# The Fourier projection unfolded, two-operand work moved from GpSimd to VectorE, and the splitting of layer 1's weights spread differently

## The chip, the cores and the metric

The kernel runs on one core of one Trainium2 chip. A core has a matrix engine (TensorE, "PE" in the profile; its weight loads are "PEld"), a vector engine (VectorE, "DVE"), an activation engine (ScalarE, "ACT"), a general engine (GpSimd, "POOL") and a queue engine that issues all transfers here (SyncE, "SP"). They run side by side and wait for one another through semaphores. Matmul results land in PSUM, eight banks of 128 x 512 float32 values; everything else is held in SBUF. The metric is the device time of one execution in microseconds (us); lower is better.

## What is computed

The program is a two-layer encoder trunk on one sequence of 512 positions and 1024 channels, in float32. Of the reference, what matters here:

```
for l in range(DEPTH):                                  # 2 layers
    h = rmsnorm(x, norm1[l])
    p = h @ w_in[l]                                     # 512 Fourier columns | 512 q | 128 k | 128 v
    f = jnp.fft.fft2(u, axes=(1, 2), norm="ortho").real # over positions and channels
    y_f = f @ w_f + b_f
    y_a = windowed_gqa(rope(rmsnorm(q)), rope(rmsnorm(k)), v, sink[l])   # 8 heads, |i-j| <= 128
    x = x + concat([rmsnorm(y_f), rmsnorm(y_a)]) @ w_o[l]
    h = rmsnorm(x, norm2[l])
    gate, val = split(dwconv_centred(h @ w_up[l], conv_w[l], conv_b[l]))  # 2 x 2816 columns
    x = x + (silu(gate) * val) @ w_down[l]
```

## The kernel before, in words

**Three matmuls for one.** Float32 operands are split into a high half that the matrix engine takes in its fast float32 form and a low half, the rest: `split` (lines 94 to 101) and `wsplit` (118 to 127) make the high half on ACT and the low half with a two-operand subtraction, by default on DVE. `mm3` (103 to 108) then issues high x high, low x high and high x low. In the profile, lines 106, 107 and 108 are these three, line 86 is any ACT instruction, line 89 any two-operand instruction of DVE or POOL, line 92 any DVE instruction with a scalar as well, since small helpers record them.

**Order.** The program is written as a plain sequence. A scheduler orders each engine's instructions by priority (program order) and by readiness in a simulation with modelled times. Only one order is written by hand: the matmuls of the first half of the output projection are issued after given steps of the attention (`proj`, line 604), as filler.

**Layer 0's mixing.** Activations are kept as eight tiles of 128 channels by 512 positions. `norm_tile` (289) scales a tile by the norm's weights and splits it, and adds its squares to an accumulator (on POOL but for the last). The q, k, v projection (325 to 346) uses these tiles as the stationary operand, in two groups of columns that both take the PSUM tags "mm" x3 and "av"; the norm's factor is put in at the eviction, a scalar for each position.

The Fourier branch uses the symmetry of a cosine and sine transform: it folds the positions (element n with element 512 - n, sums and differences) and the columns before it multiplies. `fold_h` (351) normalises a tile again, now with the factor as a row (`rb1`, line 323), folds it (`fold`, 299: a copy of two elements on DVE, a sum and a difference of 255 elements on POOL) and splits it. The weights are loaded and folded the same way (`load_wu`, 305). The projection (486 to 502) is, for each of eight channel tiles, five pieces of 256 or 258 columns, one of them with a single row. Then come the transform over channels and that over positions (526 to 557, one loop with two stages), the multiplication with the folded Fourier weights (561 to 592), a norm, and the first half of the output projection (619). The attention (436 to 476) goes head by head in 32 steps: scores, maximum on DVE, exponent on ACT, normalising on POOL, transposes on PE, split, product with v. Its result goes through the second half of the output projection (626), each of whose eight rows ends with the next norm's tile.

**Feed-forward.** 44 up projections in two halves of 22 (`HALVES`, line 35), each 24 matmuls of 512 columns with its weights loaded into one of three raw buffers ("wraw") and split, then eviction and a three-tap convolution on ACT and DVE; per pair a silu and a product (line 660, POOL). After each half the down projection: eight rows of 33 matmuls.

**Layer 1's weights ahead of time.** `presplit` (135) is a generator that runs beside layer 0's feed-forward. Each step takes one tile of layer 1's weights, folds it if it is a Fourier one, splits it and stores both halves to a scratch in DRAM. The loads use the same three raw buffers as the feed-forward's. A step is taken after each of the 44 up projections and once after each half (lines 658 and 692). In layer 1 `fetch` (183) loads the halves.

Of the kernel before, what the change touches and what calls it, by code (L numbers as in the profile page):

```python
# [37 lines left out]
def encoder_kernel(tc, t):  # L38
# [28 lines left out]
    def f(x):  # L67
# [4 lines left out]
    TEMPS = {"act": (1024, 8), "m4": (1024, 5), "slab": (1028, 4), "pT": (2560, 2),  # L72
             "tA": (512, 6), "tF": (512, 6), "sq": (512, 2)}
# [61 lines left out]
    def presplit(l):  # L135

        def keep(key, src):
# [4 lines left out]
            return lambda: [nc.sync.dma_start(o, f(z)) for o, z in zip(kept[key], two)]  # L142

        def store(waiting, w):
            if waiting:
                waiting.pop()()
            if w:
                waiting.append(w)

        late = []  # L150
        for grp in (1, 0):
            for kk in range(KT // 2):
                raw = wload(t["w_qkv"][l, grp, kk], 768)
                for i in range(2):
                    store(late, keep(f"qkv{grp}{2 * kk + i}", raw[:, i * 384:(i + 1) * 384]))
                    yield
        for kk in range(KT // 2):
            raw = wtile()
            nc.sync.dma_start(raw.rearrange("p (k c) -> p k c", k=2),
                              t["w_in"][l, 2 * kk * P:2 * (kk + 1) * P, 0:FW].rearrange("(k p) c -> p k c", p=P))  # L160
            for k in range(2):
                w = temp(512, "tA")
                fold(w, raw[:, k * 512:(k + 1) * 512], nc.vector)
                store(late, keep(f"u{2 * kk + k}", w))
                yield
        for j in range(NF):
            raw = wload(t["w_fold"][l, j], 1024)
            w = temp(512, "tA")
            tt(w[:, :256], raw[:, :256], raw[:, 512:768], ALU.add)
            tt(w[:, 256:], raw[:, 256:512], raw[:, 768:], ALU.subtract)  # L170
            store(late, keep(f"f{j}", w))
            yield
        for half in range(2):
            for mp in range(KT // 2):
                raw = wload(t["w_o"][l, half, :, mp * 1024:(mp + 1) * 1024], 1024)
                for i in range(2):
                    store(late, keep(f"o{half}{2 * mp + i}", raw[:, i * 512:(i + 1) * 512]))
                    yield
        store(late, None)
        while True:  # L180
            yield
# [65 lines left out]
    zero = temp(512, "sq")  # L247
    nc.vector.memset(zero, 0.0)
    warm = temp(512, "sq", F32R)
# [19 lines left out]
    def load_tables():  # L269
        for i in range(2):  # L270
            raw = wload(t["dft"][i], 512)
            th = cp.tile([P, 512], F32R, tag=f"th{i}", name=f"th{i}")
            tl = cp.tile([P, 512], F32R, tag=f"tl{i}", name=f"tl{i}")
            split(th, tl, raw)
            tab.append((th, tl))
        alt = wtile()[:1, :258]
# [4 lines left out]
    def add_square(acc, src, first, eng=nc.gpsimd, tag="sq"):  # L281
        if first:
            act(acc, src, AF.Square)
        else:
            sq = temp(512, tag)
            act(sq, src, AF.Square)
            tt(acc, acc, sq, ALU.add, eng)

    def norm_tile(k, g, acc):
# [3 lines left out]
        add_square(acc, x[k], k == 0, nc.gpsimd if k < KT - 1 else nc.vector)  # L293
# [5 lines left out]
    def fold(dst, src, eng):  # L299

        nc.vector.tensor_copy(dst[..., 0:257:256], src[..., 0:257:256])
        tt(dst[..., 1:256], src[..., 1:256], src[..., 511:256:-1], ALU.add, eng)
        tt(dst[..., 257:512], src[..., 1:256], src[..., 511:256:-1], ALU.subtract, eng)

    def load_wu(l, kk):

        raw = wtile()
        nc.sync.dma_start(raw.rearrange("p (k c) -> p k c", k=2),
                          t["w_in"][l, 2 * kk * P:2 * (kk + 1) * P, 0:FW].rearrange("(k p) c -> p k c", p=P))
        out = []  # L310
        for k in range(2):
            w = temp(512, "tA")
            fold(w, raw[:, k * 512:(k + 1) * 512], nc.gpsimd)
            out.append(w)
        return out
# [4 lines left out]
    for l in range(L):  # L320

        r1 = col_rstd(acc, 1.0 / D)
        rb1 = row_rstd(r1)
        qraw = {}
        for grp in (1, 0):
            pq = [psum("mm" if b < 3 else "av") for b in range(NB)]
# [22 lines left out]
        hs = {}  # L349

        def fold_h(k, eng):
            hr = temp(512, "tF")
            hf = temp(512, "tF")
            stt(hr, x[k], g1[:, l, k:k + 1], rb1, ALU.mult, ALU.mult)
            fold(hf, hr, eng)
            hs[k] = pair("slab")
            split(hs[k][:, 0, :], hs[k][:, 1, :], hf)

        for k in range(4):
            fold_h(k, nc.gpsimd)  # L360
# [4 lines left out]
        for i in range(4):  # L365
            tt(ra[:, i], ra[:, i], qkg[:, l, i, None, :].to_broadcast([P, NB, HD]), ALU.mult, nc.gpsimd)
# [5 lines left out]
        def prep(us):  # L372
# [4 lines left out]
            for i, u in enumerate(us):  # L377
                two = temp(1024, "act").rearrange("p (z b h d) -> p z b h d", z=2, **dims)
# [6 lines left out]
            for i, u in enumerate(us):  # L385
# [50 lines left out]
        def attention(p, first_pair):  # L436
# [39 lines left out]
            add_square(accA, py, first_pair, nc.vector if p == 2 else nc.gpsimd)  # L476


        if l == 0:
            load_tables()  # L480
# [4 lines left out]

        pee = [psum(), psum(), psum("av")]
        poo = psum()
        for kk in range(KT // 2):
            if not l:
                wu = load_wu(l, kk)  # L490
            for k in (2 * kk, 2 * kk + 1):
                if k not in hs:
                    fold_h(k, nc.gpsimd)
                w = fetch(f"u{k}") if l else wsplit(wu[k % 2])
                h = hs[k]
                st, sp_ = k == 0, k == KT - 1
                we = [z[:, 0:258] for z in w]
                wo = [z[:, 256:512] for z in w]
                for m, (c0, c1) in enumerate(((0, 128), (128, 256), (256, 257))):
                    mm3(pee[m][:c1 - c0, :258], [h[:, s, c0:c1] for s in range(2)], we, st, sp_)  # L500
                mm3(poo[:, 0:256], [h[:, s, 257:385] for s in range(2)], wo, st, sp_, skip_group_check=True)
                mm3(poo[:127, 256:512], [h[:, s, 385:512] for s in range(2)], wo, False, sp_, skip_group_check=True)
# [7 lines left out]
        def tail_out(pe, scale):  # L510
            b = tp.tile([1, 2, 258], F32R, tag="tail", name=nm("tail"), bufs=2)
# [3 lines left out]
        def stage_out(pe, po, scale):  # L515
            tiles = []
            for m in range(2):
                a = pair("slab", 514)
                n = P - m
                split(a[:, 0, :258], a[:, 1, :258], pe[m][:, :258], scale=scale)  # L520
                split(a[:n, 0, 258:514], a[:n, 1, 258:514], po[:n, m * 256:(m + 1) * 256], scale=scale)
# [3 lines left out]
        ue, ut = stage_out(pee, poo, 1.0)  # L525
        for stage in range(2):
            pe = [psum() for _ in range(2)]
            po = psum()
            pe.append(psum())
# [252 lines left out]
```

## Time and profile before

| | us |
|---|---|
| median of three runs | 1111.37 |
| lowest and highest of them | 1110.5, 1114.45 |
| the profiled execution | 1112.89 |
| its span, from first to last instruction | 1111.1 |
| PE busy | 1068.9 |
| DVE busy | 778.9 |
| ACT busy | 514.5 |
| POOL busy | 278.1 |

The span is one execution, recorded by the profiler. The busy time of an engine is the time in which it had an instruction under way; matmuls are pipelined and their ends modelled, so a busy PE is not necessarily at its peak rate. A group row of the profile reads: line, engine, operation, output<-inputs by the program's names, shapes, count, then busy us and mean ns of one, then the idle time of that engine just before them and what ended it.

### The profile page before, as it was taken

The page shows a single profiled execution, that of the slowest core. Times are in us where ns is not written, and L with a number is a line of the kernel's source. Part 1 is how long each engine was busy: PE and PEld are TensorE (multiplying, and loading weights), DVE is VectorE, ACT ScalarE, POOL GpSimd, SP SyncE. Part 2 cuts the span into 40 slices and gives each one's busy share as a digit, 9 for nine tenths or more (in the row PEclk, how much of TensorE's full clock was granted, in tenths as well). Part 3 has the DMA queues.
Part 4 walks back from the last instruction along what each step waited for, and adds up shares of the span by engine and source line. Part 5 has one row for each costly group of instructions (what it writes and reads, how often), then busy time and mean ns, then how long its engine had stood idle before and what let it go on. Part 6 is the DMA issues. An engine that isn't in the chain of part 4 may idle for free.

```text
span 1111.1 us, 14836 instructions
## 1 busy us (share of the span) xinstructions
PE 1068.9 (96%) x5187; PEld 892.3 (80%) x5187; DVE 778.9 (70%) x1406; ACT 514.5 (46%) x964; POOL 278.1 (25%) x326
## 2 busy tenths in 40 slices
PE   7878899999999999999999899999999999999998
PEld 6776788788888888778889787878888888888887
DVE  8997874988883477887437968477878535787732
ACT  4536763565552244554412676245555323544421
POOL 5678654511010001111105344050201000010100
PEclk9978999999999999999999999999999999999999
DMA  6312113366643576763355510523232333333241
GB/s 218 110 58 95 39 39 119 122 215 229 207 147 93 196 249 232 231 218 105 87 168 174 188 58 20 171 76 95 95 97 82 104 97 97 112 89 101 78 130 59
DMA packets 58574, 141.65 MB, mean 127 GB/s; under 512 B 6521, under 2 KB 19074, under 8 KB 58498
## 3 DMA queue, kind: packets, MB, share of 16 engines
q1 hardware_dynamic: 58498, 140.69, 40.0%
q8 instruction: 41, 0.67, 0.2%
q14 instruction: 35, 0.29, 0.1%
HBM read 117.60 MB, written 23.07 MB: 127 GB/s over the span
## 4 chain that ended last, share of the span: by engine, by line
PE 72%; DVE 15%; DMA 6%; issue 3%; ACT 2%; POOL 1%; SPq 0%; DVEq 0%; POOLq 0%; ACTq 0%
PE ps L106 22%; PE ps L108 22%; PE ps L107 22%; DVE wlo L89 4%; DMA wraw<-in_w_o_dram 3%; DMA wraw<-in_w_fold_dram 2%; DVE tF L92 2%; DVE act L89 1%; DVE act L92 1%; PE ps L450 1%; PE ps L462 1%; DVE tA L89 1%; DVE tF L89 1%; DVE slab L89 1%; DMA wraw<-in_w_in_dram 1%
## 5 line engine op out<-in xcount | busy, mean ns | idle before, releaser
L89 DVE TENSOR_TENSOR wlo<-wraw,whi 128x512 fp32r<-128x512 f32 (+1 forms) x288 | 234.6, 816 | 113.8 <-ACT whi L86 111.8
L107 PE MATMUL ps<-act,wlo 128*128 128x512 f32 x768 | 300.4, 392 | 3.7 <-DVE wlo L89 3.6
L108 PE MATMUL ps<-act,whi 128*128 128x512 f32 x768 | 300.2, 391 | 3.2 <-DVE act L92 3.1
L86 ACT ACTIVATE whi<-wraw 128x512 fp32r<-128x512 f32 (+1 forms) x300 | 183.5, 613 | 256.1 <-PE ps L108 231.7
L106 PE MATMUL ps<-act,whi 128*128 128x512 f32 x768 | 299.7, 390 | 0.0
L89 POOL TENSOR_TENSOR tF<-tF,tF 128x512 f32<-128x512 f32 x44 | 61.0, 1387 | 535.9 <-DVE tF L92 492.4
L107 PEld LDWEIGHTS ps<-act,wlo 128*128 128x128 f32 x768 | 144.6, 188 | 36.2 <-DVE wlo L89 6.2
L108 PEld LDWEIGHTS ps<-act,whi 128*128 128x128 f32 x768 | 144.6, 188 | 35.5 <-DVE act L92 6.1
L106 PEld LDWEIGHTS ps<-act,whi 128*128 128x128 f32 x768 | 144.5, 188 | 30.2
L92 DVE SCALAR_TENSOR_TENSOR tF<-tF,pb,tF 128x511 f32<-128x511 f32 x176 | 132.8, 759 | 8.7 <-ACT tF L86 5.5
L89 DVE TENSOR_TENSOR tF<-ps,rb 128x512 f32<-128x512 f32 x104 | 70.6, 686 | 43.8 <-PE ps L108 32.6
L106 PE MATMUL ps<-slab,whi 128*128 128x512 f32 (+2 forms) x228 | 87.3, 383 | 1.0 <-ACT slab L86 1.0
L107 PE MATMUL ps<-slab,wlo 128*128 128x512 f32 (+2 forms) x228 | 85.2, 374 | 0.0
L108 PE MATMUL ps<-slab,whi 128*128 128x512 f32 (+2 forms) x228 | 84.9, 375 | 0.1
L86 ACT ACTIVATE tF<-tF,pb 128x512 f32<-128x512 f32 x88 | 71.5, 815 | 15.7 <-DVE tF L89 12.3
L89 DVE TENSOR_TENSOR x<-x,ps 128x512 f32<-128x512 f32 (+1 forms) x49 | 33.0, 676 | 46.1 <-PE ps L108 46.1
L89 POOL TENSOR_TENSOR acc<-acc,sq 128x512 f32<-128x512 f32 x28 | 43.0, 1535 | 60.0 <-ACT sq L86 59.3
L107 PE MATMUL ps<-pT,wlo 128*128 128x512 f32 (+1 forms) x132 | 51.0, 386 | 0.0
L108 PE MATMUL ps<-pT,whi 128*128 128x512 f32 (+1 forms) x132 | 50.8, 385 | 0.0
L106 PE MATMUL ps<-pT,whi 128*128 128x512 f32 (+1 forms) x132 | 50.8, 385 | 0.0
L106 PEld LDWEIGHTS ps<-slab,whi 128*128 128x128 f32 x228 | 42.9, 188 | 8.8 <-ACT slab L86 1.4
L108 PEld LDWEIGHTS ps<-slab,whi 128*128 128x128 f32 x228 | 42.8, 188 | 8.5 <-DVE slab L89 0.4
(171 smaller groups left out, 1791.3 us busy)
## 6 DMA issues: line engine op xcount, KB each, us to landing
wraw<-in_w_up_dram SPq DMA_DIRECT2D x88, 512.0 KB, 3.8
wraw<-in_w_down_dram SPq DMA_DIRECT2D x32, 512.0 KB, 3.5
kept<-tA SPq DMA_DIRECT2D x56, 256.0 KB, 4.3
wraw<-in_w_o_dram SPq DMA_DIRECT2D x16, 512.0 KB, 3.6
whi<-kept SPq DMA_DIRECT2D x28, 256.0 KB, 3.5
wlo<-kept SPq DMA_DIRECT2D x28, 256.0 KB, 3.7
wraw<-in_w_qkv_dram SPq DMA_DIRECT2D x16, 384.0 KB, 3.5
kept<-tA SPq DMA_DIRECT2D x32, 192.0 KB, 2.1
```

Of the source, the lines that this page charges most:

```text
L86: return nc.scalar.activation(out, in_, func, **kw)
L89: return (eng or nc.vector).tensor_tensor(out, a, b, op=op)
L92: return nc.vector.scalar_tensor_tensor(out=out, in0=a, scalar=s, in1=b, op0=op0, op1=op1)
L106: nc.tensor.matmul(out, a[0], b[0], start=start, stop=False, **kw)
L107: nc.tensor.matmul(out, a[1], b[0], start=False, stop=False, **kw)
L108: nc.tensor.matmul(out, a[0], b[1], start=False, stop=stop, **kw)
L450: nc.tensor.matmul(sc[:, :n], qT[p][:, e, i * P:(i + 1) * P], kT[g][:, s, j0 * P:(j1 + 1) * P], start=s == 0, stop=s == 1)
L462: tr = nc.tensor.transpose(pp[:, j * P:(j + 1) * P], pr[:, j * P:(j + 1) * P], ident)
```

## The change

Four things change together.

1. The Fourier projection is not folded. It takes the tiles `xg` that the q, k, v projection uses, so the output is positions by columns: four PSUM tiles of 512 columns, 12 matmuls for each channel tile. The columns alone are folded, on the result, with the norm's factor as a scalar for each position (`fold`, now an ACT copy, a two-element DVE instruction and two DVE ones of 255). `fold_h` and `rb1` go. The channel transform sums over four tiles of 128 positions, with two more table tiles made by copies with alternating sign; the sine part has a row of zeros so that all pieces have 128 rows. The tables are loaded before the projection.
2. Two-operand POOL instructions go to DVE: square sums, rotary products, low halves of layer 0's output and Fourier weights, their folds, four residual additions, and layer 0's gate product. Layer 1's gate product stays on POOL, as do the normalising and a one-column copy in the attention.
3. The second q, k, v group uses other PSUM banks, and `prep` takes "slab" temporaries; the "sq" buffers go.
4. `presplit` loads into "m4" buffers, a job ahead, without folding the Fourier projection's weights; the Fourier weights load without their duplicate quarter pair. A step is taken after every third up projection and two before each row of the down projection: 7 + 16 in each half.

```diff
+        if l == 0:
+            load_tables()
+        pu = [psum("mm" if b < 3 else "av") for b in range(NB)]
+        for kk in range(KT // 2):
+            raw = None if l else load_wu(l, kk)
+            for k in (2 * kk, 2 * kk + 1):
+                w = fetch(f"u{k}") if l else wsplit(raw[:, (k % 2) * 512:(k % 2 + 1) * 512])
+                for b in range(NB):
+                    mm3(pu[b], [xg[k][:, s, b * P:(b + 1) * P] for s in range(2)], w, k == 0, k == KT - 1)
+        ub = []
+        for b in range(NB):
+            uf = temp(512, "tF")
+            fold(uf, pu[b], r1[:, b:b + 1])
+            a = pair("act")
+            split(a[:, 0, :], a[:, 1, :], uf)
+            ub.append(a)
...
+    def fold(dst, src, scale):
+
+        up = temp(256, "tF")
+        act(up[:, :255], src[:, 257:512], scale=scale)
+        nc.vector.tensor_scalar(dst[:, 0:257:256], src[:, 0:257:256], scale, None, op0=ALU.mult)
+        stt(dst[:, 1:256], src[:, 1:256], scale, up[:, 254::-1], ALU.mult, ALU.add)
+        stt(dst[:, 257:512], src[:, 1:256], scale, up[:, 254::-1], ALU.mult, ALU.subtract)
...
-            pq = [psum("mm" if b < 3 else "av") for b in range(NB)]
+            pq = [psum(("mm", "mm", "mm", "av")[b] if grp else ("sc", "sc", "tp", "tp")[b]) for b in range(NB)]
...
-        add_square(acc, x[k], k == 0, nc.gpsimd if k < KT - 1 else nc.vector)
+        add_square(acc, x[k], k == 0)
...
-                       ropeB[isk][:, :, None, d0:d0 + 32].to_broadcast([P, NB, 2, 32]), ALU.mult, nc.gpsimd)
+                       ropeB[isk][:, :, None, d0:d0 + 32].to_broadcast([P, NB, 2, 32]), ALU.mult)
...
-            return wchunks(t["w_o"][l, half, :, mp * 1024:(mp + 1) * 1024], 1024, eng=nc.gpsimd)
+            return wchunks(t["w_o"][l, half, :, mp * 1024:(mp + 1) * 1024], 1024)
...
-                tt(x[m], x[m], ts, ALU.add, nc.gpsimd if m < 4 else nc.vector)
+                tt(x[m], x[m], ts, ALU.add)
...
-                    next(ahead)
+                    if (2 * n + z) % 3 == 2:
+                        next(ahead)
                 act(ys_[0], ys_[0], AF.Silu)
-                tt(ys_[0], ys_[0], ys_[1], ALU.mult, nc.gpsimd)
+                tt(ys_[0], ys_[0], ys_[1], ALU.mult, nc.gpsimd if l else nc.vector)
...
             for m in range(KT):
+                next(ahead)
+                next(ahead)
...
+        got = jobs[0][0]()
+        for n, (_, keys) in enumerate(jobs):
+            for i, key in enumerate(keys):
+                keep(key, fold_w(got[i]) if key[0] == "f" else got[i])
+                if i == len(keys) - 1 and n + 1 < len(jobs):
+                    got = jobs[n + 1][0]()
+                yield
```

More of the change, by code (lines that the diff above doesn't have):

```diff
@@ L141, in keep, with store @@
             kept[key] = [dp.tile([P, n], F32, tag=f"{key}{s}", name=nm("kept")) for s in range(2)]
[L142 to L150, printed above, removed]
+            store()
+            late.append(lambda: [nc.sync.dma_start(o, f(z)) for o, z in zip(kept[key], two)])
+        def store():
+            while late:
+                late.pop()()
@@ L161, in presplit @@
[L161 to L165, printed above, removed]
-        for j in range(NF):
[L167 to L172, printed above, removed]
+            jobs.append((lambda kk=kk: wu(kk), [f"u{2 * kk + i}" for i in range(2)]))
@@ L173, in presplit @@
+        for j in range(NF):
+            jobs.append((lambda j=j: [load_wf(l, j, temp(1024, "m4"))], [f"f{j}"]))
         for half in range(2):
             for mp in range(KT // 2):
[L175 to L179, printed above, removed]
+                jobs.append((cols(t["w_o"][l, half, :, mp * 1024:(mp + 1) * 1024], 1024, 512),
+                             [f"o{half}{2 * mp + i}" for i in range(2)]))
```

200 lines of the change are left out of this document (88 added, 112 removed).

## The prediction, made before the result was known

> **What bounds the kernel now.** I began with the page's first part, for which engine is nearly full.
>
> ```profile
> PE 1068.9 (96%) x5187; PEld 892.3 (80%) x5187; DVE 778.9 (70%) x1406; ACT 514.5 (46%) x964; POOL 278.1 (25%) x326
> ```
>
> PE is busy for 96% of the span, but this average hides two kinds of stage. So I asked next for the busy time by stretches, cut where the listing of PE's instructions changes: layer 0 until PE starts to run without breaks on the output projection (0 to 140 us), a stretch of layer 0's up projection (235 to 360), one of its second up projection (420 to 500), layer 1's mixing up to the attention half of its output projection (573 to 716), and a short one that holds only folded Fourier projection matmuls (623.4 to 629.2).
>
> ```profile
> core 0: us, PE busy (x) PEld busy (x) DVE busy (x) ACT busy (x) POOL busy (x), PEclk, DMA share, GB/s
> 0.00:140.00 140.00, 113.97 (x668) 99.24 (x668) 122.35 (x272) 78.85 (x183) 97.99 (x128) 0.91 0.31 103
> 140.00:172.00 32.00, 31.34 (x175) 26.85 (x176) 22.55 (x62) 19.90 (x49) 16.88 (x27) 1.00 0.13 38
> 235.00:360.00 125.00, 125.00 (x550) 102.96 (x549) 95.41 (x154) 61.79 (x103) 15.30 (x11) 1.00 0.54 171
> 420.00:500.00 80.00, 76.32 (x330) 61.21 (x329) 65.40 (x92) 42.40 (x70) 11.40 (x12) 1.00 0.70 230
> 573.00:716.00 143.00, 137.38 (x860) 121.44 (x860) 103.40 (x283) 71.50 (x182) 51.68 (x89) 1.00 0.38 122
> 623.40:629.20 5.80, 5.80 (x51) 5.48 (x50) 5.13 (x7) 0.97 (x2) 4.57 (x5) 1.00 0.80 249
> ```
>
> The third row gives PE's price of a 512-column matmul without waits: 125 us / 550 = 0.227 us. The last row gives that of a 256- or 258-column one: 5.8 us over 51, of which about two straddle the edges, so 0.118 us. In the first row PE idles 26 us and DVE is the fullest engine: 122.35 of 140, 87%, with POOL at 98 us beside it. From 140 to 172 us PE is full and DVE has 9 us of slack. So layer 0's mixing is limited by DVE with its POOL partner up to 140 us and by PE after that. Layer 1's mixing is close to PE-bound: 137.4 of 143. The feed-forward is PE-bound except for 420 to 500, where PE did 330 matmuls, worth 330 x 0.227 = 74.9 us, in 80.
>
> Then I asked for layer 0's DVE and POOL groups, shapes kept apart, in 0 to 140 us.
>
> ```profile
> L89 DVE TENSOR_TENSOR wlo<-wraw,whi 128x384 fp32r<-128x384 f32 x16 | 13.2, 851 | 0.4 <-PE ps L108 0.3
> L92 DVE SCALAR_TENSOR_TENSOR tF<-x,pa,rb 128x512 f32<-128x512 f32 x8 | 8.6, 1079 | 0.1
> L89 DVE TENSOR_TENSOR slab<-tF,slab 128x512 fp32r<-128x512 f32 x8 | 7.6, 975 | 0.0
> L92 DVE SCALAR_TENSOR_TENSOR act<-x,pa,act 128x512 fp32r<-128x512 f32 x8 | 7.3, 928 | 1.6 <-ACT act L86 1.6
> L89 DVE TENSOR_TENSOR wlo<-tA,whi 128x512 fp32r<-128x512 f32 x8 | 7.1, 887 | 0.0
> ...
> L89 DVE TENSOR_TENSOR act<-act,ropetab 128x512 f32<-128x512 f32 x5 | 5.1, 1023 | 0.0
> L89 DVE TENSOR_TENSOR m<-act,m 128x512 fp32r<-128x512 f32 x6 | 4.8, 804 | 0.0
> L89 DVE TENSOR_TENSOR act<-act 128x512 f32<-128x512 f32 x5 | 4.3, 855 | 0.1
> L89 DVE TENSOR_TENSOR pT<-ps,pT 128x384 fp32r<-128x384 f32 x8 | 4.2, 544 | 0.0
> L301 DVE COPY tF<-tF 128x2 f32<-128x2 f32 x8 | 4.0, 496 | 0.0
> ...
> L301 DVE COPY tA<-wraw 128x2 f32<-128x2 f32 x8 | 3.1, 425 | 0.0
> L89 DVE TENSOR_TENSOR tF<-tF,ps 128x255 f32<-128x255 f32 x8 | 3.0, 410 | 1.2 <-PE ps L108 1.2
> ```
>
> ```profile
> L89 POOL TENSOR_TENSOR tF<-tF 128x255 f32<-128x255 f32 x16 | 15.1, 966 | 14.8 <-DVE tF L92 14.8
> L89 POOL TENSOR_TENSOR tA<-wraw 128x255 f32<-128x255 f32 x16 | 14.3, 923 | 0.5 <-DMA wraw<-in_w_in_dram 0.5
> L89 POOL TENSOR_TENSOR wlo<-wraw,whi 128x512 fp32r<-128x512 f32 x9 | 13.1, 1457 | 6.8 <-ACT whi L86 6.8
> L89 POOL TENSOR_TENSOR act<-act,ropetab 128x256 f32<-128x256 f32 x10 | 10.1, 1036 | 1.4 <-DVE act L89 1.4
> L89 POOL TENSOR_TENSOR acc<-acc,sq 128x512 f32<-128x512 f32 x6 | 9.3, 1542 | 4.3 <-ACT sq L86 4.0
> L89 POOL TENSOR_TENSOR ropetab<-ropetab,pb 128x256 f32<-128x256 f32 x8 | 7.1, 917 | 1.9 <-DMA ropetab<-in_rope_dram 1.9
> L89 POOL TENSOR_TENSOR wraw<-wraw 128x256 f32<-128x256 f32 x8 | 7.0, 899 | 0.0
> ...
> L89 POOL TENSOR_TENSOR accF<-accF,tF 128x512 f32<-128x512 f32 x3 | 3.8, 1283 | 0.1
> ```
>
> The reader is to compare shapes. Over the whole trace a 512-element DVE instruction with one operand in PSUM takes 0.686 us:
>
> ```profile
> L89 DVE TENSOR_TENSOR tF<-ps,rb 128x512 f32<-128x512 f32 x104 | 70.6, 686 | 43.8 <-PE ps L108 32.6 <-ACT rb L86 11.1
> ```
>
> Those with both operands in SBUF take 0.80 to 1.08 us while POOL works; a 384-element one takes 0.851, against 0.544 with an operand in PSUM. So POOL's work slows DVE's.
>
> **The change part by part. Fourier projection on PE.** Before, each of the 8 channel tiles has 15 matmuls of 256 or 258 columns (the one-row piece streams as many columns as the others): 15 x 0.118 = 1.77 us. After, 12 of 512: 2.72 us. Eight tiles: +7.6 us per layer. The channel transform goes from 24 matmuls with 258 columns (six of them the tail's) and 12 with 256 to 36 and 24: 24 more, +2.8 us. The position transform and the projection after it keep their counts. The row broadcast rb1 goes: eight matmuls of 128 columns, at most 8 x 0.118 = 0.9 us. So PE gets +9.5 us of work per layer.
>
> **Layer 0's mixing, DVE.** Removed by rows: the normalised copies 8.6, their low halves 7.6, the two-element copies 4.0 and 3.1, and one set of eviction halves, five of about 0.41, 2.0: 25.3 us. POOL's two fold rows (29.4 us) disappear outright. Moved from POOL to DVE, at 0.686 us for 512 elements and 0.41 for 256: nine low halves 6.2, ten rotary products 4.1, six square sums 4.1, eight rotary tables 3.3, eight folds of the Fourier weights 3.3, three square sums of its output 2.1. New: four folds of the projection, each two of 255 elements, one of 512 and a two-element one (0.82 + 0.69 + 0.42, the last at the dearer rows' price): 7.7. Together 30.8 us. Relief of what stays: 16 x (851 - 544) + 8 x (928 - 686) + 8 x (887 - 686) + 5 x (1023 - 686) + 6 x (804 - 686) + 5 x (855 - 686) ns = 4.9 + 1.9 + 1.6 + 1.7 + 0.7 + 0.8 = 11.6 us. DVE's need is 122.35 - 25.3 + 30.8 - 11.6 = 116.3 us, 6 less than now.
>
> The Trainium skill, SBUF — State Buffer, section "Who interferes with whom", says that a DVE instruction with two SBUF inputs contends with a GpSimd one that reads SBUF, and that the loser is fully blocked. By that lock the relief could reach, as an estimate from the page, the POOL rows above (79.8 us) times the share of DVE's time in such instructions (about 0.47): 37 us instead of 11.6, and layer 0 some 25 us shorter than I forecast; the trace agrees on which shapes are slowed and shows only the smaller sum, which I use.
>
> How much of the 140 us this returns depends on how full DVE then is. At today's 87% it is 116.3 / 0.874 = 133 us, a gain of 7. At 93% it is 125, a gain of 15. I take 11, nearer neither end: PE's big wait, for the chain of normalising on DVE, folding on POOL, splitting on ACT and DVE before a Fourier matmul can run, is gone, since the unfolded projection reads the tiles that the q, k, v projection has used already; but the attention's chain of score, exp, normalise and transpose stays. PE's extra 9.5 us lies in this stretch's 26 us of idle time; if that cover is gone it costs itself. The transform tables load earlier, in five pieces instead of two, ahead of the first Fourier weights on SP's queue and in the three raw buffers, with eight more ACT copies; the cover is the second half of the q, k, v projection. Without it PE would wait for one load, whose price stands with the feed-forward below. The q group now has score and transpose banks of PSUM, so it need not wait for the first group's eviction; that is in the gain. In the second half of the output projection DVE takes the additions of POOL and their low halves; PE fills with the next up projections, so I book +1 us there.
>
> **Layer 1's mixing.** PE's +9.5 meets 143 - 137.4 = 5.6 us of visible idle. If all of it is filled, +4; if none, +9.5; PE busy is modelled, so waits shorter than a matmul hide in it, which could be won too: then -1. I take +2: the projection is now 22 us of PE work without a wait inside, beside which the attention's preparation can run on a DVE that has lost its normalising and folding, about 20 us as in layer 0's rows.
>
> **Layer 0's feed-forward.** In the second up projection the chain of waits repeats one pattern:
>
> ```profile
> 437.36 3.71 DMA wraw<-in_w_o_dram
> 449.28 3.57 DMA wraw<-in_w_o_dram
> 461.08 3.62 DMA wraw<-in_w_o_dram
> 467.34 1.70 DVE wlo L89
> 472.93 3.89 DMA wraw<-in_w_o_dram
> ```
>
> A load of layer 1's weights comes every 11.86 us, (472.93 - 437.36) / 3, while two up projections need 48 x 0.227 = 10.9. The load waits for one of three raw buffers shared with the up weights, and ACT and DVE stand behind it. After, these loads have buffers of their own, are asked for a step ahead, and only every third up projection carries a split. DVE there also loses the folds and gains 22 products, 22 x 0.686 = 15 us in some 240. The excess of 80 - 74.9 = 5.1 us goes: -5. What is late next is PE itself. In the down projection each of the 8 rows now carries two splits; DVE gains 2 x 0.686 = 1.4 us and ACT about as much, against a PE time of 33 x 0.227 = 7.5, so I cost it at nothing, with a rival below. In the first half a row's second split may read a tile asked for just before it: ACT then stands up to 3.9 us, with that row's weight halves queued behind it on ACT and DVE, and PE waits only if the halves made ahead, five pairs of buffers, run out. Layer 1's product stays on POOL, where PE is already full: nothing.
>
> Sum: -11 + 1 + 2 - 5 = -13 us. The profiled execution took 1112.89 us (span 1111.1), 1.5 above the median of 1111.37; I take the change from the median: 1098 us.
>
> **The rivals.** *PE is the bound.* If PE's idle in 0 to 140 us belongs to the attention chain and not to the folding, its busy share stays at 114 / 140: layer 0 costs 9.5 / 0.81 = +11.7, layer 1 +9.5, the feed-forward -5: 1128 us. It decides as soon as less than 9 us of layer 0's PE idle can be filled. For it: layer 1 is nearly full already. Against it: the fold chain is what DVE does just when PE is emptiest.
>
> *DVE gets fuller.* If POOL's neighbours do not get faster, DVE needs 127.9 us, 146 at its present share: +6; the output projection +3, layer 1 +2, feed-forward -5: 1117 us, at the edge of what can be told from no change. The Trainium skill, Perfetto Trace Analysis, section "Optimizing Scalar/DVE Operations", says that when DVE is saturated, offloading to GPSIMD may make sense, with the doubt that the two share a port; it speaks against moving work here, and the slowed rows above speak against it.
>
> *Both stretches close up.* With DVE at 98% in layer 0, as full as PE is from 140 to 172 us, it takes 119 us, -21; layer 1 -1; feed-forward -5: 1084 us.
>
> *Transfers bind in the down projection.*
>
> ```profile
> wraw<-in_w_down_dram SPq DMA_DIRECT2D x32, 512.0 KB, 3.5
> kept<-tA SPq DMA_DIRECT2D x56, 256.0 KB, 4.3
> wraw<-in_w_o_dram SPq DMA_DIRECT2D x16, 512.0 KB, 3.6
> ```
>
> Each row moves 704 KB of down weights (512 and a piece three eighths as big) and, for two splits, 512 KB in and four times 256 KB out: 2.24 MB in 7.5 us, 299 GB/s, where 249 at a share of 0.80 is the most shown. Scaled by share it just fits (0.96). If 249 is the limit, a row takes 9.0 us: +1.5 for some ten rows, 15 us, and the sum is 1113.
>
> **How the numbers follow.** Forecast 0.45, closed up 0.20, DVE fuller 0.15, PE bound 0.13, transfers 0.07. The forecast's own range is 1088 to 1109: layer 0 between 7 and 15, layer 1 between -1 and +9.5. A measurement here can tell 0.5% (5.6 us) from no change. Faster: nearly all of the forecast, the closed case and a little of the transfers, 0.65. Same: most of the transfers, half of the DVE case and the forecast's edge, 0.17. Slower: PE bound and the other half of the DVE case, 0.18 with the edges. The range takes in the closed case with a margin for more relief, and the DVE case with its edge: 1073 to 1119.
>
> **What would show it.** Right: PE's first Fourier matmuls follow the last q, k, v matmul without a gap; no L301 copies of two elements; two-SBUF DVE rows near 0.69 us in layer 0; the feed-forward starts about 11 us earlier in layer 0; 48 matmuls per 10.9 us in layer 0's second up projection. Wrong: DVE idle in the mixing while PE is stalled on attention waits, a down-projection row over 7.5 us, or layer 1's mixing more than 5 us longer than now.

## The result: 1.1% slower, and what the profile shows

The changed kernel takes 1124.35 us, median of four runs (1124.02 to 1124.9), against 1112.05 for the kernel before (also of four; the 1111.37 above is that of three of them): a ratio of 1.0109, 95% interval 1.009 to 1.0129. 1098 was forecast, with a range to 1119. The profiled execution took 1124.26 us.

First the page's first part, which answers to the first line shown of before.

```profile
span 1122.5 us, 14711 instructions
...
PE 1081.3 (96%) x5171; PEld 912.8 (81%) x5171; DVE 755.4 (67%) x1476; ACT 520.5 (46%) x960; POOL 84.1 (7%) x159
```

POOL has lost 194 us of work and DVE, which took much of it over, has become emptier, not fuller. PE's share is the same. Nothing here says why the kernel is slower. So next the stretches, the first four cut as before; the fifth is again 143 us from the start of layer 1, and the last is a part of the unfolded Fourier projection.

```profile
core 0: us, PE busy (x) PEld busy (x) DVE busy (x) ACT busy (x) POOL busy (x), PEclk, DMA share, GB/s
0.00:140.00 140.00, 122.58 (x714) 107.25 (x714) 112.96 (x325) 91.82 (x220) 31.02 (x73) 0.99 0.36 120
140.00:172.00 32.00, 25.41 (x106) 22.00 (x107) 17.43 (x57) 10.88 (x23) 0.00 (x0) 0.66 0.12 40
235.00:360.00 125.00, 125.00 (x553) 103.52 (x552) 93.15 (x144) 63.45 (x100) 0.00 (x0) 1.00 0.44 141
420.00:500.00 80.00, 80.00 (x355) 66.24 (x354) 59.41 (x88) 39.46 (x58) 0.00 (x0) 1.00 0.30 95
568.00:711.00 143.00, 129.65 (x768) 116.86 (x767) 86.06 (x282) 67.54 (x172) 21.94 (x59) 0.94 0.31 97
44.00:65.00 21.00, 21.00 (x94) 17.34 (x94) 20.31 (x54) 11.35 (x22) 0.00 (x0) 1.00 0.36 106
```

Much of the forecast is there. The projection runs without a break (94 matmuls in 21 us). The feed-forward's second up projection is full: 355 matmuls in 80 us, 330 before. From 0 to 140 us PE does 714 matmuls instead of 668, the larger ones of the projection among them. But from 140 to 172, where PE was full before, it is idle for 6.6 us, at a granted clock of 0.66, and layer 1's stretch holds 768 matmuls where before it held 860. Cut closer around that place, the same is seen in each layer:

```profile
136.00:162.00 26.00, 16.39 (x71) 14.98 (x69) 14.69 (x52) 9.67 (x20) 0.00 (x0) 0.54 0.25 90
687.00:713.00 26.00, 17.46 (x77) 15.81 (x75) 11.52 (x46) 7.09 (x15) 0.00 (x0) 0.64 0.19 61
```

Against the first of these, 26 us of the kernel before:

```profile
136.00:162.00 26.00, 24.53 (x144) 21.05 (x143) 21.98 (x64) 19.74 (x52) 15.18 (x31) 1.00 0.13 42
```

No engine is full in these 26 us: PE does 71 matmuls where it did 144, DVE has 11 us to spare. Something waits for something. What runs there is told by the listings of single tiles. In these rows stand line, engine, operation, output<-inputs, count, shortest, median and longest duration in ns, then the start of the first and of the last in us. Of the kernel after, layer 0, the tile tF:

```profile
L86 ACT ACTIVATE tF<-ps,pa x4: 470/477/481, 139.6 to 150.9; 128x258 f32<-128x258 f32 x4
...
L89 DVE TENSOR_TENSOR acc<-acc,tF x3: 693/693/851, 118.2 to 139.8; 128x512 f32<-128x512 f32 x3
```

The first row is the eviction behind the folded Fourier weights' matmuls (line 585), the second the sum of the attention's squares (line 306). The evictions begin with the last square. Of the kernel before, the first square sum of the Fourier output, and the attention's last one:

```profile
L86 ACT ACTIVATE accF<-tF x1: 613/613/613, 111.6 to 111.6; 128x512 f32<-128x512 f32 x1
```

```profile
L89 DVE TENSOR_TENSOR acc<-acc,sq x1: 685/685/685, 175.9 to 175.9; 128x512 f32<-128x512 f32 x1
```

There the Fourier branch's last part began 64 us ahead of the attention's last sum and ran beside the attention. Now it comes behind it. In order of time, where the two meet in the kernel after (start us, duration us, what; in brackets the engine's idle time before it and what ended that):

```profile
139.13 0.60 ACT L86 ACTIVATE tF<-ps 128x512 f32<-128x512 f32 x1 [0.41 <-DVE act L92]
139.62 0.47 ACT L86 ACTIVATE tF<-ps,pa 128x258 f32<-128x258 f32 x1
...
140.14 0.58 PE L106 MATMUL ps<-slab,whi 128*128 128x256 f32 x1 [3.91 <-ACT tF L86]
```

The attention's last square at 139.13 takes a tF buffer; the Fourier tail's first eviction follows half a microsecond later, and PE, idle for 3.91 us, is let go by it. The tail's first two evictions had their sums ready long before: PE's last matmul for each stands at 98 and 101 us.

```profile
97.75 0.28 PE L108 MATMUL ps<-tail,wt 1*128 1x258 f32 x1
...
101.06 0.28 PE L108 MATMUL ps<-tail,wt 1*128 1x258 f32 x1
```

The attention is now done 36 us earlier than before (139.8 against 175.9), but the Fourier weights, the norm of their result and only then the first half of the output projection follow one by one, where the output projection had been the attention's filler.

From PE's listing comes the length of each stage. A feed-forward's start is taken as that of its 241st matmul less 240 x 0.227 us, since its first ones are interleaved with the mixing; the other marks are layer 1's first projection matmul and the end:

| us | before | after | E1 | E6 |
|---|---|---|---|---|
| layer 0's mixing | 206.1 | 208.9 | 195.3 | 187.1 |
| layer 0's feed-forward | 367.0 | 359.1 | 359.1 | 359.1 |
| layer 1's mixing | 173.0 | 191.6 | 179.0 | 171.2 |
| layer 1's feed-forward | 365.1 | 362.9 | 363.0 | 362.9 |
| span | 1111.1 | 1122.5 | 1096.3 | 1080.3 |

The last two columns are experiments of the next section.

### The profile page after: what moved, and what is told of

Its sections match the earlier page's. It is cut to its first block, busy times and chain, and to the rows that moved or that the text cites. A ratio compares the mean times of both kernels' runs of the same rounds, so it can differ in the third digit from the quotient of the medians.

```text
span 1122.5 us, 14711 instructions
## 1 busy us (share of the span) xinstructions
PE 1081.3 (96%) x5171; PEld 912.8 (81%) x5171; DVE 755.4 (67%) x1476; ACT 520.5 (46%) x960; POOL 84.1 (7%) x159
## 5 line engine op out<-in xcount | busy, mean ns | idle before, releaser
L86 ACT ACTIVATE whi<-wraw 128x512 fp32r<-128x512 f32 (+1 forms) x308 | 188.5, 616 | 309.8 <-PE ps L108 287.4
L89 DVE TENSOR_TENSOR wlo<-wraw,whi 128x512 fp32r<-128x512 f32 (+1 forms) x316 | 227.8, 724 | 99.3 <-ACT whi L86 95.8
L106 PE MATMUL ps<-slab,whi 128*128 128x512 f32 (+2 forms) x228 | 89.0, 391 | 7.6 <-ACT tF L86 6.5
L108 PE MATMUL ps<-slab,whi 128*128 128x512 f32 (+2 forms) x228 | 87.1, 385 | 0.3 <-DVE slab L89 0.3
L106 PE MATMUL ps<-whi,act 128*128 128x384 f32 (+1 forms) x192 | 66.6, 355 | 1.6 <-ACT whi L86 1.6
L107 PE MATMUL ps<-whi,act 128*128 128x384 f32 (+1 forms) x192 | 67.4, 354 | 0.0
L108 PE MATMUL ps<-wlo,act 128*128 128x384 f32 (+1 forms) x192 | 63.1, 353 | 0.0
L106 PEld LDWEIGHTS ps<-slab,whi 128*128 128x128 f32 x228 | 45.9, 201 | 17.2 <-ACT tF L86 6.9
L89 POOL TENSOR_TENSOR tF<-tF,tF 128x512 f32<-128x512 f32 x22 | 30.1, 1369 | 349.8 <-DVE tF L92 327.4
L493 POOL TENSOR_SCALAR tA<-tA,den 128x256 f32<-128x256 f32 (+1 forms) x64 | 40.8, 644 | 160.6 <-DVE den L492 160.2
L108 PEld LDWEIGHTS ps<-slab,whi 128*128 128x128 f32 x228 | 45.6, 200 | 8.3 <-DVE slab L89 0.7
```

What stands on the lines that cost most here:

```text
L86: return nc.scalar.activation(out, in_, func, **kw)
L89: return (eng or nc.vector).tensor_tensor(out, a, b, op=op)
L106: nc.tensor.matmul(out, a[0], b[0], start=start, stop=False, **kw)
L107: nc.tensor.matmul(out, a[1], b[0], start=False, stop=False, **kw)
L108: nc.tensor.matmul(out, a[0], b[1], start=False, stop=stop, **kw)
L493: nc.gpsimd.tensor_scalar(pr[:, :n], pr[:, :n], den[:, i:i + 1], 1.0, op0=ALU.mult, op1=ALU.mult)
```

## The experiments

A tag names a small set of buffers that temporaries of one kind share. Each ratio below is to the kernel before as measured beside that run, whose medians were 1112.62 to 1114.18 us; differences between two experiments are of their medians.

Theory A: one edit that the prediction passed over, the attention's squares moved from the tag "sq" to the tag "tF". The Fourier tail takes its temporaries from tF too, and stands behind the attention in the program. If the buffers of a tag are given out in the program's order, the tail can't have one until the last square has. Rival B: the 9.5 us of PE work added per layer are the bound. Rival C: the first splits of layer 1's weights, which now have buffers of their own to load into, run early, in layer 0's attention, and hold it up.

**E1: the squares in another tag.**

```diff
-            add_square(accA, py, first_pair)
+            add_square(accA, py, first_pair, "tA")
```

> The kernel after, with one edit: the attention's squares take a temporary of the tag tA instead of tF. Theory A (the buffers of a tag are given out in program order, so the Fourier tail's tF temporaries wait for the last attention pair's square, and PE has nothing to do for about 26 us between the end of the attention and the output projection, in each layer): the Fourier weights' matmuls move back among the attention's steps, the gap closes in both layers, and about 10 to 15 us come back per layer: 1095 to 1105 us. Rival B (PE's added 9.5 us per layer are the bound): 1120 to 1124, since PE's work is unchanged. Theory C (the hoisted splits of layer 1's weights hold up ACT in layer 0's attention): layer 1 gains nothing, layer 0 little, 1117 or more.

1098.76 us; ratio to before 0.9864 (0.9849 to 0.9879). One word takes 25.6 us off the changed kernel. The table gives 13.6 to layer 0's mixing and 12.6 to layer 1's, as theory A had it. B and C are out as main causes.

**E2: the same cause put into the kernel before.**

```diff
-            add_square(accA, py, first_pair, nc.vector if p == 2 else nc.gpsimd)
+            add_square(accA, py, first_pair, nc.vector if p == 2 else nc.gpsimd, tag="tF")
```

> The kernel before, with the attention's squares in the tag tF instead of sq; nothing else. Theory A: the Fourier tail is put behind the attention here too and the same gap opens in both layers; 1125 to 1140 us against 1112. Rival B (PE's added work) and theory C: nothing that they speak of is touched, 1112 within 3 us.

1152.23 us, ratio 1.0341 (1.0323 to 1.0359): slower by 38 us, more than expected, with layer 0's mixing at 228.2 us and layer 1's at 190.9. Its first Fourier square moves from 111.6 us to behind the attention's last sum, which here starts at 156.2:

```profile
L86 ACT ACTIVATE accF<-tF x1: 613/613/613, 158.4 to 158.4; 128x512 f32<-128x512 f32 x1
```

So the cause needs nothing else of the change.

**E3: layer 1's splits later.** E1, and the splits wait for the row factor that ends layer 0's mixing.

```diff
+        behind = last[0]
...
-            split(two[0], two[1], src)
+            with tc.issue_after(behind.ins):
+                split(two[0], two[1], src)
...
-        act(rb, pt)
+        last[0] = act(rb, pt)
```

> E1, and the splits of layer 1's weights may not be issued ahead of the norm's row factor that ends layer 0's mixing. Theory C (the first splits, hoisted into layer 0's attention, take tA buffers and ACT's queue there): 5 to 8 us below E1. Theory A alone: within 2 us of E1.

1096.52 us, ratio 0.9838 (0.982 to 0.9856): 2.2 below E1, all of it in layer 0's mixing (193.1 against 195.3). Theory C has a price, but a small one.

**E4: the moved work back on POOL**, with E1's tag.

```diff
-                tt(x[m], x[m], ts, ALU.add)
+                tt(x[m], x[m], ts, ALU.add, nc.gpsimd if m < 4 else nc.vector)
...
-            return wchunks(t["w_o"][l, half, :, mp * 1024:(mp + 1) * 1024], 1024)
+            return wchunks(t["w_o"][l, half, :, mp * 1024:(mp + 1) * 1024], 1024, eng=nc.gpsimd)
```

and so on, for each instruction of the change's second part.

> E1, with all the two-operand work that the change moved to DVE given back to POOL (square sums, rotary products, folds and low halves of the Fourier weights, low halves of the output weights, four residual additions, layer 0's gate product). If the moving pays by freeing DVE's partner in SBUF, as the prediction had it: 8 to 20 us above E1. If DVE was not the limit of the mixing: within 3 us of E1.

1110.93 us, ratio 0.9976 (0.9961 to 0.999): 12 us above E1, 8.1 in layer 0's mixing and 3.6 in layer 1's. The moving pays.

**E5 and E6: the number of buffers, or their order?** Both get room for one more 512-element buffer by holding one row factor instead of two. E5 gives it to tF; E6 makes it a tag for the attention's squares alone.

```diff
-             "tA": (512, 5), "tF": (512, 6)}
+             "tA": (512, 5), "tF": (512, 7)}
```

> The kernel after, with the tag tF given seven buffers instead of six (the room comes from the row factor rb, two buffers to one); the attention's squares stay in tF. If the Fourier tail waits because tF has too few buffers: part of the gap closes, 1100 to 1118 us. If it waits because the buffers of one tag are given out in program order, whatever their number: within 3 us of the kernel after, 1124.

```diff
-             "tA": (512, 5), "tF": (512, 6)}
+             "tA": (512, 5), "tF": (512, 6), "sq": (512, 1)}
...
-            add_square(accA, py, first_pair)
+            add_square(accA, py, first_pair, "sq")
```

> The same room used in another way: tF keeps six buffers and the attention's squares get one buffer of a tag of their own, sq. If the order within the tag is the cause: near E1, 1094 to 1101 us, from as much memory as the run with seven tF buffers. If the number of buffers is the cause: no better than that run.

E5: 1124.17 us, ratio 1.0093 (1.0062 to 1.0124), no gain at all over the change. E6: 1081.53 us, ratio 0.9709 (0.9673 to 0.9746), 17 below E1 and better than expected. From the same memory the one gives nothing and the other 43 us, so it is the order in the tag and not the one buffer more; more than seven tF buffers were not tried. In the tile listings the first Fourier square starts at 145.0 us in E5,

```profile
L86 ACT ACTIVATE accF<-tF x1: 613/613/613, 145.0 to 145.0; 128x512 f32<-128x512 f32 x1
```

and at 100.9 in E6:

```profile
L86 ACT ACTIVATE accF<-tF x1: 612/612/612, 100.9 to 100.9; 128x512 f32<-128x512 f32 x1
```

Why E1 was not as good is seen in its own trace in order of time, where the attention goes from one pair of heads to the next. E1's squares share tA with the attention's probabilities, whose tiles begin with line 487, which puts an extra column in:

```profile
116.40 0.48 POOL L487 COPY tA<-nsink 128x1 f32<-128x1 f32 x2 [1.14 <-PE ps L496]
...
120.78 0.60 ACT L86 ACTIVATE tA<-ps 128x512 f32<-128x512 f32 x1 [0.82 <-DVE act L92]
...
121.75 0.69 DVE L89 TENSOR_TENSOR acc<-acc,tA 128x512 f32<-128x512 f32 x1
...
122.50 0.18 POOL L487 COPY tA<-nsink 128x1 f32<-128x1 f32 x1 [5.62 <-DVE acc L89]
```

Four probability tiles of the next pair had begun from 114 to 117 us. The fifth comes only behind the square sum, since the square holds one of the five tA buffers; POOL waits for such a sum twice in layer 0, 10.6 us in all. Here the number of buffers may count as well: the change also takes tA from six buffers to five, which neither its description nor the prediction names, and no run puts the sixth back. In E6 the stretch that was empty is full, and so is layer 1's:

```profile
136.00:162.00 26.00, 26.00 (x135) 21.99 (x134) 19.34 (x44) 15.68 (x35) 3.72 (x7) 1.00 0.54 175
```

```profile
546.00:689.00 143.00, 140.46 (x843) 125.63 (x842) 92.40 (x283) 69.65 (x176) 25.16 (x59) 1.00 0.38 120
```

**E7 and E8: what freed the feed-forward.** E1 with the loads of layer 1's weights back in the three raw buffers (E7), and E1 with the old schedule, a split after each up projection, but loads in the new buffers (E8).

```diff
-                raw = temp(1024, "m4")
+                raw = wtile()
```

> E1, with the loads of layer 1's weights beside layer 0's feed-forward taken back into the three raw buffers of the up and down weights; their schedule stays the new one. If the shared raw buffers were what cost the second up projection (as the prediction had it): layer 0's feed-forward is 4 to 8 us longer, 1103 to 1107 us. If it was the schedule, a split after each up projection: within 2 us of E1.

```diff
-                    if (2 * n + z) % 3 == 2:
-                        next(ahead)
+                    next(ahead)
...
-                next(ahead)
-                next(ahead)
```

> E1, with the old schedule of those splits, one after each up projection and one after each half, and their loads in the m4 buffers as in the change. If the shared raw buffers were the cost: within 2 us of E1. If the schedule was: layer 0's feed-forward 4 to 8 us longer, 1103 to 1107 us.

E7: 1099.16 us (ratio 0.987, 0.9837 to 0.9903), the same as E1. E8: 1103.39 (0.9908, 0.9874 to 0.9943), 4 to 5 more. But in both the feed-forward takes E1's 359 us, and E8's loss lies ahead of it, in the last part of layer 0's mixing and the first up projections (202.5 against 195.3 by the same mark). So either edit alone is enough to remove the waits in the second up projection: neither a load after each up projection nor the shared raw buffers brings them back by itself. That the two together do was not run; the kernel before, which has both and the waits, also folds in these splits and asks for no load a step ahead. What E8 pays early was not taken apart.

**E9 to E12: on top of E6.** E9 adds E3's edit.

> The squares in a buffer of their own (E6), and the splits of layer 1's weights not ahead of the row factor that ends layer 0's mixing (E3). If the early splits cost by themselves, about 2 us, as E3 took from E1: 1079 to 1080. If they only cost where tA buffers are short, within 1 us of E6's 1081.5.

1081.88 us, ratio 0.9718 (0.9703 to 0.9732): no gain that shows. The early splits cost something beside E1's squares in tA, and nothing here.

E10 adds E4's edit.

> E6 with the moved two-operand work back on POOL, as in E4. The prediction's relief (11.6 us of DVE time in layer 0's mixing, turned into about as much time): 8 to 14 us above E6, 1090 to 1095. If the moving pays only where tA holds the attention up: within 3 us of E6. If DVE has room and POOL's extra engine is worth more: below E6.

1098.53 us, ratio 0.9866 (0.9851 to 0.988): 17.0 above E6; by stages 11.8 in layer 0's mixing and 2.7 in layer 1's, in a profiled execution that was the fastest of the four (1096.72). DVE's own instructions are slow again, from 0 to 140 us:

```profile
L89 DVE TENSOR_TENSOR wlo<-wraw,whi 128x384 fp32r<-128x384 f32 x16 | 11.1, 719 | 0.4 <-PE ps L108 0.3
...
L92 DVE SCALAR_TENSOR_TENSOR act<-x,pa,act 128x512 fp32r<-128x512 f32 x8 | 8.3, 1060 | 1.7 <-ACT act L86 1.6
```

E11 adds PE work to the projection:

```diff
+                    for _ in range(9 if k == 0 else 0):
+                        nc.tensor.matmul(pu[b], xg[k][:, 0, b * P:(b + 1) * P], w[0], start=True, stop=True)
```

> E6 with nine idle copies of the first matmul of each of the Fourier projection's four accumulations, whose result the real ones overwrite: 36 matmuls of 512 columns, 36 x 0.227 = 8.2 us of PE work more per layer, about as much as the change added. Rival B (PE is the bound): 16 us above E6, 1098. The prediction's terms (layer 0 hides it, layer 1 pays a part): 2 to 9 us, 1084 to 1090.

1094.98 us, ratio 0.9838 (0.9822 to 0.9855): 13.5 above E6, of 16.4 added; by stages 4.7 of 8.2 in layer 0's mixing and 8.1 of 8.2 in layer 1's. Nearer to B than to the prediction's terms.

E12 takes the q group's own PSUM banks away:

```diff
-            pq = [psum(("mm", "mm", "mm", "av")[b] if grp else ("sc", "sc", "tp", "tp")[b]) for b in range(NB)]
+            pq = [psum("mm" if b < 3 else "av") for b in range(NB)]
```

> E6 with the q group of the projection back on the PSUM banks of the k and v group. If the other banks saved a wait at the turn from one group to the next, PE waits there for four evictions of ACT and four of DVE, 3 to 6 us per layer: 1087 to 1093. If not: within 2 us of E6.

1088.48 us, ratio 0.9783 (0.9767 to 0.9799): 7 us. PE's waits from 20 to 50 us name the eviction of the value columns, the last of the first group:

```profile
PE ps L106 <- DVE vz L92: 5.5, 1, 5.5
```

**E13 and E14: what was left of the feed-forward.** It had gained more than the waits of one up projection, and layer 1's, which carries no splits, 2 us. In the kernel before, 512-column matmuls that read slab, pT or m tiles in the down projection start 229 to 235 ns apart, in the kernel after 227; the diff makes the slab buffers 1024 elements long instead of 1028. E13 puts that back alone, E14 takes another size.

```diff
-    TEMPS = {"act": (1024, 8), "m4": (1024, 5), "slab": (1024, 4), "pT": (2560, 2),
+    TEMPS = {"act": (1024, 8), "m4": (1024, 5), "slab": (1028, 4), "pT": (2560, 2),
```

> E6 with the slab buffers of 1028 elements, as in the kernel before, instead of 1024; what is computed and its order on every engine stay as in E6. In the kernel before, 512-column matmuls that read slab, pT or m tiles start 229 to 235 ns apart, in the kernel after 227, while those that read act tiles have 227 in both. If the slab size does it, by where it puts the tiles behind it in SBUF: the down projections are about 2 us longer in each layer, 229 to 235 ns again in these rows, and the time is 4 to 6 us above E6, 1085 to 1088. If the row times come from what runs beside the matmuls (POOL's work, the old splits): E6's 1081.5 within 1.5 us.

> E6 with the slab buffers of 1040 elements: bigger again, but by a multiple of 64 bytes. If the place of the tiles within 64 bytes matters: 227 ns apart and E6's time, within 1.5 us. If any other size than 1024 costs: as E13.

E13: 1086.38 us, ratio 0.9757 (0.9734 to 0.978). E14: 1083.84, ratio 0.9735 (0.9712 to 0.9759). As ratios these can't be told from E6 with certainty, but the traces can: the feed-forwards take 361.5 and 365.1 us in E13, 360.5 and 364.0 in E14, 359.1 and 362.9 in E6. The same 50 us of the down projection in E13, E14 and E6:

```profile
835.00:885.00 50.00, 50.00 (x218) 40.67 (x217) 21.50 (x32) 13.79 (x23) 1.29 (x1) 1.00 0.33 98
```

```profile
835.00:885.00 50.00, 50.00 (x220) 41.02 (x219) 21.32 (x31) 13.97 (x23) 1.29 (x1) 1.00 0.33 97
```

```profile
835.00:885.00 50.00, 50.00 (x222) 41.42 (x221) 19.69 (x30) 13.60 (x24) 1.70 (x1) 1.00 0.32 97
```

In layer 1's down projection the matmuls that read high halves from slab, pT and m tiles start 231, 231 and 234 ns apart in E13 (medians), in E14 233, 227 and 227, in E6 227. Both expectations of E14 were half right: its slab tiles are slow too, its m tiles are not, and its pT tiles are in between (the same median is 231 in layer 0).

The best version is E6: the change with one buffer of its own for the attention's squares, 2.9% faster than the kernel before.

## Why the prediction was wrong

**The failed step** is in "Layer 0's mixing" and "Layer 1's mixing": the -11 + 1 and the +2. They measured +2.8 and +18.6. Both were worked out of engine loads: DVE's need went down and the gain was taken from how full DVE would be. That the "sq" buffers go was told as a part of the change, but was costed nowhere, not even at nothing with the work that hides it. The step lacked the question who else takes buffers of the tag that the squares move to, and whether those tiles come later in the program. With the squares out of tF the same two terms measure -10.8 and +6.0 (E1), or -19.0 and -1.8 (E6). E1, E2, E5 and E6 show the cause.

**The sum without it.** E1 has 1098.76 us, the forecast 1098; that they agree so well owes something to chance, as the terms are not of their size: layer 1's mixing cost 4 us more than forecast and the two feed-forwards gave 5 us more. E6 has 1081.5, near the rival *Both stretches close up* (1084), but not for that rival's reason, which was a DVE 98% full in layer 0. From 0 to 140 us in E6:

```profile
0.00:140.00 140.00, 129.23 (x750) 113.85 (x751) 115.92 (x341) 90.46 (x214) 31.50 (x69) 1.00 0.32 107
```

DVE is busy for 83% of it, less than the 87% of before, and PE for 92%. So to work the gain out of how full DVE would become was off here too, where the squares share no tag. A part that no term had is the granted clock, 0.91 in this row before and 1.00 in E6.

**The relief of DVE** was right. From 0 to 140 us in the kernel after:

```profile
L89 DVE TENSOR_TENSOR wlo<-wraw,whi 128x512 fp32r<-128x512 f32 x14 | 9.6, 682 | 1.7 <-PE ps L108 1.5
...
L89 DVE TENSOR_TENSOR wlo<-wraw,whi 128x384 fp32r<-128x384 f32 x16 | 8.2, 548 | 2.1 <-ACT whi L86 2.1
...
L92 DVE SCALAR_TENSOR_TENSOR act<-x,pa,act 128x512 fp32r<-128x512 f32 x8 | 5.9, 742 | 1.5 <-ACT act L86 1.5
...
L89 DVE TENSOR_TENSOR m<-slab,m 128x512 fp32r<-128x512 f32 x6 | 3.9, 672 | 0.0
...
L89 DVE TENSOR_TENSOR slab<-slab,ropetab 128x512 f32<-128x512 f32 x5 | 3.3, 660 | 0.0
...
L89 DVE TENSOR_TENSOR slab<-slab 128x512 f32<-128x512 f32 x5 | 3.2, 659 | 0.0
```

Against the durations of before that is 16 x 303 + 8 x 186 + 8 x 205 + 5 x 363 + 6 x 132 + 5 x 196 ns = 11.6 us, the same as forecast (two shapes came out a little dearer, the rest cheaper). The two-element copies of the folding are gone. The rival *DVE gets fuller* falls with it, and so say E10's 17 us, at 1.06 us for an instruction of 0.742: giving work to GpSimd here makes DVE slower. The Trainium skill, Perfetto Trace Analysis, "Optimizing Scalar/DVE Operations", says that offloading work of a saturated DVE to GPSIMD may make sense, but might not help, as the two share a port; E10 bears out the doubt. The prediction's estimate from the Trainium skill, SBUF — State Buffer, "Who interferes with whom", of 37 us of relief and 25 us in layer 0 beyond the forecast, was too much: the relief measured 11.6, and E6 is 9 us below the forecast's 1 - 11 there.

**PE's added work.** The prediction hid all 9.5 us of it in layer 0 and 7.5 in layer 1. E11 shows that on top of E6 about 60% of PE work added at this place counts in layer 0 (4.7 of 8.2 us) and all of it in layer 1. The rival *PE is the bound* had this right; it was wrong in the sign of the whole, since the waits that the unfolding and the moving removed are worth more.

**The feed-forward.** -5 was forecast, -7.9 measured. The step itself was right in place and size: from 420 to 500 us there are 355 matmuls, 25 more than before, worth 5.7 us. That either of two edits is enough (E7, E8) it did not see. The rest, and the 2.1 us of layer 1's feed-forward, which was put at nothing, are the slab buffers' size, 2.4 and 2.2 us by E13 against E6: a second small line of the diff without a price.

**Transfers in the down projection** did not bind, though near it. From 322 to 380 us:

```profile
322.00:380.00 58.00, 58.00 (x257) 48.05 (x256) 34.39 (x59) 25.65 (x45) 0.00 (x0) 1.00 0.85 298
```

257 matmuls in 58 us is full speed, at 298 GB/s, so the 249 of that rival was no limit.

**Its own signs.** Of what was to show it wrong, one came true word for word: layer 1's mixing is 18.6 us longer. The signs of it being right came true too, but for layer 0's earlier feed-forward. Signs of single steps can't show a step that is missing.

## What to carry to other kernels

A temporary's tag can act as a queue in the order of the program: before a tile moves to another tag, list who takes that tag later in the program but should run earlier, for they may come to wait for it, and one buffer more need not help (E5). A change of many parts is costed part by part from the diff, the smallest line too; here the dearest was a tag in a helper's default argument. When an engine is full because of its neighbour, taking the neighbour's work over can make room, and the durations of the slowed instructions say how much.

## What the runs showed of the hardware that was not expected

Where a matmul's moving operand lies in SBUF has a price: 512 columns take 227 ns from one place and up to 234 from another (E6, E13, E14; what each engine does, and in which order, is the same in the three). That it is the start address is read from the sizes of the buffers; no trace shows an address, and E14's pT tiles, slow in one layer more than in the other, leave open what about the place counts.

A gap costs more than its idle time, as the granted clock falls in it. Stretches of the kernel after:

```profile
130.00:136.00 6.00, 4.46 (x26) 3.17 (x24) 3.42 (x8) 2.97 (x7) 0.58 (x1) 1.00 0.64 229
136.00:141.00 5.00, 1.09 (x7) 0.89 (x6) 3.54 (x8) 3.25 (x7) 0.00 (x0) 0.67 0.78 280
141.00:150.00 9.00, 9.00 (x40) 8.32 (x40) 5.26 (x13) 3.68 (x8) 0.00 (x0) 0.50 0.15 48
150.00:158.00 8.00, 2.65 (x11) 2.30 (x11) 4.67 (x30) 1.84 (x4) 0.00 (x0) 0.50 0.17 62
162.00:166.00 4.00, 3.35 (x13) 2.47 (x14) 4.00 (x7) 2.37 (x5) 0.00 (x0) 1.00 0.00 0
```

After the wait of 3.91 us the clock stands at 0.50, and the next 40 matmuls, 32 of them the Fourier weights', of 258 columns and fewer, take 9 us instead of some 40 x 0.118 = 4.7. In E6 the same stretch had the full clock. The Trainium skill, TensorE: Matmul & The Clock Gate, Part 1, says that an idle window of about 3.4 us sets the array to half rate and a busy one of that length sets it back. This trace agrees only in part. The wait began at 136.23 (140.14 - 3.91), and by the 0.67 of the row from 136 to 141 us the clock fell at about 137.7: 1.5 us without work were enough, behind a stretch in which PE was busy for 4.46 of 6 us. The way back took longer: 0.50 still stands from 150 to 158 us, after 9 us that are recorded as busy. The recorded busy time is modelled, so short pauses within it may be the reason; no run here shows it.

Transfers reached 365 GB/s at a share of 1.02 from 170 to 185 us of E8, where 249 at 0.80 was the most that the prediction had quoted:

```profile
170.00:185.00 15.00, 15.00 (x76) 12.65 (x75) 10.28 (x28) 7.21 (x13) 0.00 (x0) 1.00 1.02 365
```
